# Dealing recombinations and end sums out over units in a hybrid decoder layer

## The chip, the core and the metric

The kernel runs on one core of one Trainium2 chip. A core has a matrix engine (PE), a vector engine (DVE), a scalar engine (ACT), GpSimd (POOL) and a queue engine (SP); POOL and SP issue the DMAs here. The metric is device time in microseconds of one launch, the median of the runs. Lower is better.

## What is computed

One layer of a decoder over 272 positions (16 learned ones and 256 of the sequence) of width 2048, all in float32: a half-step feed-forward block, a mixer (sparse attention beside a short gated convolution), and a second half-step feed-forward block. The change touches the two gates of the mixer and the second feed-forward block:

```python
merged = sigmoid(ga) * y_attn + sigmoid(gc) * y_conv      # ga, gc: columns of u @ w_in
h = h + merged @ w_out
u = rms_norm(h, ffn2_norm_g)
h = h + 0.5 * (silu(u @ w_gate) * (u @ w_up)) @ w_down    # width 5632
return h[:, N_META:]
```

## The kernel before

**Two parts, one stream.** All weights are read once, in the order of their use, by an object `Stream` (`st`). It cuts them into units of at most 1024 float32 columns on 128 partitions. For each unit ACT makes a rounded high part (`whi`, L202) and DVE the rest (`wlo`, L203), so that a product in float32 is three fp32r matmuls (L577 to L579). `st.next()` opens a unit. In this order it runs the functions registered by `st.early` that are due, then `st.split`, which makes the high and low parts of the unit five ahead, and then what was registered by `st.later(fn, lag)`; a lag of 1 is the unit that is opened next (or the one being opened, when the call comes from an early function). Each engine works its own instructions in the order in which the program issues them, so this order is the order of DVE's queue.

**Pairs and banks.** From the gates on (from about 1100 us) a stage is a `group`: 256 tokens against 512 columns of two matrices (gate and up, or two column blocks of the down matrix). The contraction runs over pairs of 128-row blocks. A plain pair (kind `C`) makes 8 block products in two units, 24 matmuls: the first unit (`plain_half`) adds to the PSUM banks q2 and q3, the second to q4 and q8; `hook(n)` stands between the two. A seven-product pair (kind `S` or `D`) makes 7 products in 21 matmuls over four units of 2, 2, 2 and 1 blocks, in the order of banks q7, q5, q6, q3, q1, q4, q2. Sums of weights that it needs (`sb`, L180 and L181) are made on DVE by `sum_ahead`, inside `st.split`, six units ahead. For kind `D` a part of these sums is made by an accumulating DMA that POOL issues (L149). All eight PSUM banks are in use.

**The end of a group.** When the last seven-product pair of a group is over, `recombine` is due at the next unit: ACT copies q1 (`va`, L654), and DVE makes `vv`, `vx`, `vv` again and `ve` from q6, q7, q5 and q5 (L655 to L658), all before that unit's split. That unit is called U0 below. When the last pair is over, `after_end` is due: it adds the plain banks to these (four DVE sums over q2, q3, q4, q8), and what follows depends on the group.

- Gates (`gates`, four groups): four sums (L1131), four sigmoids on ACT.
- `up_group` (eleven groups, g = 0 to 10): four sums in the order q3, q4, q2, q8 (L1270), two SiLU on ACT (L1272), the products (L1277) one unit later. The products are turned by eight PE transposes (`turn_mid`, `turn_four`, L624) into banks and copied out as `mid`. This happens at the hook of pair 6 of the next up group (banks q1 and q5), or at pair 1 of the down group (q6 and q1).
- `down_group`, twice a half: the output `ht` (two tiles of 128 tokens by 2048) takes half of each recombined tile (`after_seven`, four DVE operations L1301, at U0 right behind `recombine`) and half of each bank (four more L1301 in `after_end`). In the last group the output DMAs (L1312) follow.

The plan is up 0 to 3, down, up 4 to 7, down, up 8 to 10, down. The kinds of an up group are `CCCDCDCC` for g = 0 and `DCDCDCCC` else; a half of a down group has `CCDCDCDC` (four up groups) or `CCDCDC` (three), the same in both halves.

**The start of the second block.** In up group 0 the residual `h` is turned to token rows by eight groups of four transposes (`turn_h`, L1251), each into a bank that ACT copies out (L1252): two at the hook of pair 0, four at pair 1, two at pair 2. `norm2` at pair 2 puts the sums of squares into bank q6.

Of the kernel before, what the change touches and what calls it, by code (L numbers as in the profile page):

```python
# [12 lines left out]
ALU = mybir.AluOpType  # L13
# [242 lines left out]
def tile_decoder_layer(  # L256
# [61 lines left out]
            st.add(wo[d, :, a * P : b * P], b - a, P)  # L318
    chunks(wo, SIDE, KD)
    for kind, at in PLAN:  # L320
        for k in [p[0] for p in (pairs_up(at) if kind == "up" else pairs_down(at) * 2)]:
            st.add_pair(k, w2_c, w2_d)

    const.tile([P, 32], F32, name="lead")
# [294 lines left out]
    def turn_four(to, m, tags, extra=None):  # L619

        for j in range(NT):
            ps = bank(tags[j], "pt")
            for f in range(4):
                nc.tensor.transpose(ps[:, f * P : (f + 1) * P], m[j][:, f * P : (f + 1) * P], ident)  # L624

            def after(j=j, ps=ps):
                cols = slice(j * P, (j + 1) * P)
                src = ps.rearrange("p (f t) -> p f t", f=4)
                for a, b, x in to:
                    split_into(x[:, :, 0, cols], x[:, :, 1, cols], src[:, a:b, :])  # L630
                if extra:
                    extra(src, cols)

            st.later(after)

    def group(todo, hook, after_seven, after_end):
# [12 lines left out]
        buf = {}  # L649

        def recombine():
            a, v, x, e = (small_tile(n) for n in "avxe")
            buf.update(q2=a, q3=v, q4=x, q8=e)
            nc.scalar.activation(a, q["q1"][0], AF.Copy)  # L654
            nc.vector.tensor_sub(v, q["q6"][0], a)  # L655
            nc.vector.tensor_add(x, q["q7"][0], v)
            nc.vector.tensor_sub(v, q["q5"][0], v)
            nc.vector.scalar_tensor_tensor(e, q["q5"][0], -1.0, x, op0=ALU.mult, op1=ALU.add)  # L658
            after_seven(buf)

        for n, (kind, four, ts) in enumerate(todo):
            b11, b12, b21, b22 = four()
            if kind != "C":
                t1, t3, t2, t4 = (both(ts()[:, :, f * P : (f + 1) * P]) for f in range(4))
                for tag, t in (
                    ("q7", t3), ("q5", t1), ("q6", t2), ("q3", b22), ("q1", b11), ("q4", t4), ("q2", b21)
                ):
                    mac3(of(tag), t, st.next())
                if n == last:
                    st.early(recombine)  # L670
            else:
                plain_half(b11, b12, b21, b22, of("q2"), of("q3"))
                hook(n)
                plain_half(b11, b12, b21, b22, of("q4"), of("q8"))
        st.early(lambda: after_end(q, buf))

    with ExitStack() as mix:
        a_hi, a_lo = parts(LATER)
# [445 lines left out]
        def gates(c):  # L1124

            box = {}

            def after_end(q, buf):
                box.update(buf)
                for tag in ("q2", "q3", "q4", "q8"):  # L1130
                    nc.vector.tensor_add(buf[tag], q[tag][0], buf[tag])  # L1131
                for n, tag in enumerate(("q2", "q3", "q4", "q8")):
                    j = 1 + n % 2
                    nc.scalar.activation(buf[tag], buf[tag], AF.Sigmoid, scale=rcol[:, 2 * j : 2 * j + 1])
# [77 lines left out]
    def turn_mid(tags):  # L1212
# [3 lines left out]
        g, m = waiting.pop(0)  # L1216
        to = right[0][:, slot[g]]
        mids[g] = to
        ks = [f // 2 for k, gg, f in pairs_down(part[g]) if gg == g and k != "C"]
        if ks:  # L1220
            x = small_tile("m1").rearrange("p (i t) -> p i t", i=2)

# [31 lines left out]
    def up_group(g):  # L1254

        def hook(n):
            if g == 0:
                if n == 0:
                    st.later(lambda: nc.vector.tensor_add(ssq[0][:, META:], ssq[0][:, META:], ssq[1][:, META:]))
                if n == 2:  # L1260
                    norm2()
                if n < 3:
                    for i, tag in zip(((0, 1), (2, 3, 4, 5), (6, 7))[n], ("q1", "q5", "q6", "q7")):
                        turn_h(i // 2, i % 2, tag)
            elif n == 6:
                turn_mid(("q1", "q5"))

        def after_end(q, buf):
            for tag in ("q3", "q4", "q2", "q8"):
                nc.vector.tensor_add(buf[tag], q[tag][0], buf[tag])  # L1270
            for j, tag in enumerate(("q2", "q3")):
                nc.scalar.activation(buf[tag], buf[tag], AF.Silu, scale=r2[:, 2 * j : 2 * j + 1])  # L1272

            def products():
                m = [small_tile(f"m{j}") for j in range(NT)]
# [7 lines left out]

        group(
            [(k, lambda i=i: four_of(act2, 2 * i, 2 * i + 1), lambda i=i: made[i]) for k, i in pairs_up(g)],
            hook, lambda buf: None, after_end,
        )

    PLACES = {"q2": (0, 0), "q3": (1, 0), "q4": (0, 1), "q8": (1, 1)}

    def down_group(gs, final):
        pairs = pairs_down(gs)
        for half in range(2):

            def place(tag, half=half):
# [4 lines left out]
            def add_half(to, x):  # L1300
                nc.vector.scalar_tensor_tensor(to, x, 0.5, to, op0=ALU.mult, op1=ALU.add)  # L1301

            def after_seven(buf, place=place):
                for tag in PLACES:
                    add_half(place(tag)[2], buf[tag])

            def after_end(q, buf, place=place):
                for tag in ("q3", "q4", "q2", "q8"):
# [5 lines left out]
            group(  # L1314
                [
                    (k, lambda g=g, f=f: four_of(mids[g], f, f + 1), lambda g=g, f=f: made_mid[g, f])
                    for k, g, f in pairs
                ],
                lambda n: n == 1 and half == 0 and turn_mid(("q6", "q1")), after_seven, after_end,
            )  # L1320

    right = []
# [63 lines left out]
def _second(wg, wu, wd):  # L1386
    res = []
    for kind, at in PLAN:
        if kind == "up":
            res += [_quads(k, wg, wu, i, at, at) for k, i in pairs_up(at)]  # L1390
        else:
            res += [
                _quads(k, wd, wd, 2 * g + f // 2, 2 * m, 2 * m + 1) for m in range(2) for k, g, f in pairs_down(at)
            ]
    return _both_kinds(res)

# [81 lines left out]
```

## Time and profile before

| | |
|---|---|
| median of 3 runs | 2197.49 us (2193.02 to 2199.24) |
| profiled execution, its own time | 2201.74 us |
| its span | 2200.0 us |
| mean granted PE clock in it | 0.991 |
| DVE, ACT, POOL busy | 1503.8, 1080.3, 82.3 us |
| weights and inputs read | 431.29 MB, 197 GB/s over the span |

The profile gives times from the start of the span. A row of the timeline reads: start, duration, engine, line, operation, output tile<-input tiles, shape, count, and in brackets the idle time of the engine before it with what ended it. A row of the windows view has the busy time and, in brackets, the number of instructions of each engine in a stretch, then the clock that PE was granted and the DMA engines' busy share. Ends of matmuls are modelled, so PE's pace is read from the number of matmuls in a window rather than from its busy time.

### The profile page before, as it was taken

Reading aid. Unit: us, or ns where it says so; the run is one execution under the profiler, and the core shown is the slowest. Engines: PE = TensorE matmul, PEld = TensorE weight load, DVE = VectorE, ACT = ScalarE, POOL = GpSimd, SP = SyncE. Lnnn points to the kernel's source line nnn. Section 1 sums busy time; section 2 is a strip of 40 time slices with the busy share of each in tenths; the row PEclk is TensorE's granted clock in tenths of the full one; section 3 lists DMA queues with packets and bytes.
Section 4 is the critical chain, followed back from the end, with each engine's and each line's share of the span. In section 5 each row is a group of like instructions: output and inputs, shape, how many; then the busy total and the mean of one; then the engine's idle time right before and its main releaser. Section 6 shows DMA issues by size and latency. Waiting matters only on the chain.

```text
span 2200.0 us, 32155 instructions
## 1 busy us (share of the span) xinstructions
PE 2143.0 (97%) x13045; PEld 1926.7 (88%) x13045; DVE 1503.8 (68%) x1918; ACT 1080.3 (49%) x1397; POOL 82.3 (4%) x94
## 2 busy tenths in 40 slices
PE   8999999999999999999999999999998999989997
PEld 8999999999999998889988888888877787777876
DVE  7555544455555555686677885778877887778876
ACT  6444433344444445564455554666554565545643
POOL 2000000000000000000000000100000000000000
PEclk9999999999999999999999999999999999999999
DMA  6555555555545555443555555578777877778764
GB/s 238 190 178 187 173 176 183 178 172 180 185 173 175 184 175 175 153 163 128 179 202 198 187 208 172 192 240 255 240 232 231 253 241 236 221 228 256 239 221 122
DMA packets 77765, 435.48 MB, mean 198 GB/s; under 512 B 8656, under 2 KB 8784, under 8 KB 36912
## 3 DMA queue, kind: packets, MB, share of 16 engines
q1 hardware_dynamic: 70416, 407.67, 52.7%
q0 software_dynamic: 7056, 25.59, 6.9%
q8 instruction: 102, 1.67, 0.3%
q14 instruction: 47, 0.39, 0.0%
q10 hardware_dynamic: 144, 0.17, 0.0%
HBM read 431.29 MB, written 2.10 MB: 197 GB/s over the span
## 4 chain that ended last, share of the span: by engine, by line
PE 85%; DVE 8%; ACT 2%; DMA 2%; issue 1%; POOL 1%; SPq 0%; DVEq 0%; ACTq 0%; POOLq 0%
PE q L577 11%; PE q L578 11%; PE q L579 11%; PE pd L372 4%; PE pd L371 4%; PE pd L373 4%; PE pu L371 4%; PE pg L371 4%; PE pg L373 4%; PE pu L373 4%; PE pu L372 4%; PE pg L372 4%; DVE wlo L203 3%; DMA raw<-in_w2d_dram 2%; ACT whi L202 2%; PE po L386 1%
## 5 line engine op out<-in xcount | busy, mean ns | idle before, releaser
L203 DVE TENSOR_TENSOR wlo<-raw,whi 128x1024 fp32r<-128x1024 f32 (+1 forms) x752 | 903.7, 1208 | 607.5 <-ACT whi L202 591.2
L202 ACT ACTIVATE whi<-raw 128x1024 fp32r<-128x1024 f32 (+1 forms) x752 | 782.8, 1044 | 858.8 <-PE q L579 187.8
L577 PE MATMUL q<-whi,act 128*128 128x512 f32 x833 | 327.1, 393 | 8.0 <-DVE vv L1270 4.1
L578 PE MATMUL q<-wlo,act 128*128 128x512 f32 x833 | 325.5, 391 | 0.8 <-DVE wlo L203 0.8
L579 PE MATMUL q<-whi,act 128*128 128x512 f32 x833 | 325.0, 390 | 0.0
L371 PE MATMUL pd<-mid,whi 128*128 128x272 f32 x704 | 201.7, 287 | 0.0
L372 PE MATMUL pd<-mid,whi 128*128 128x272 f32 x704 | 201.7, 287 | 0.0
L373 PE MATMUL pd<-mid,wlo 128*128 128x272 f32 x704 | 201.7, 287 | 0.0
L577 PEld LDWEIGHTS q<-whi,act 128*128 128x128 f32 x833 | 157.0, 188 | 42.5 <-DVE vv L1270 5.4
L371 PE MATMUL pg<-act,whi 128*128 128x272 f32 x672 | 192.7, 287 | 0.0
L372 PE MATMUL pu<-act,whi 128*128 128x272 f32 x672 | 192.5, 287 | 0.0
L373 PE MATMUL pg<-act,wlo 128*128 128x272 f32 x672 | 192.5, 287 | 0.0
L371 PE MATMUL pu<-act,whi 128*128 128x272 f32 x672 | 192.5, 287 | 0.0
L372 PE MATMUL pg<-act,whi 128*128 128x272 f32 x672 | 192.5, 287 | 0.0
L373 PE MATMUL pu<-act,wlo 128*128 128x272 f32 x672 | 192.5, 287 | 0.0
L578 PEld LDWEIGHTS q<-wlo,act 128*128 128x128 f32 x833 | 157.0, 188 | 33.6 <-DVE wlo L203 1.9
L579 PEld LDWEIGHTS q<-whi,act 128*128 128x128 f32 x833 | 156.9, 188 | 32.9
L577 PE MATMUL q<-whi,mid 128*128 128x512 f32 x272 | 111.5, 410 | 29.9 <-DVE ht L1301 20.5
L371 PEld LDWEIGHTS pd<-mid,whi 128*128 128x128 f32 x704 | 132.6, 188 | 0.0
L372 PEld LDWEIGHTS pd<-mid,whi 128*128 128x128 f32 x704 | 132.6, 188 | 0.0
L373 PEld LDWEIGHTS pd<-mid,wlo 128*128 128x128 f32 x704 | 132.6, 188 | 0.0
L371 PEld LDWEIGHTS pg<-act,whi 128*128 128x128 f32 x672 | 126.6, 188 | 0.0
(289 smaller groups left out, 3777.7 us busy)
## 6 DMA issues: line engine op xcount, KB each, us to landing
raw<-in_wgu_dram SPq DMA_DIRECT2D x87, 1024.0 KB, 4.8
raw<-in_w_dram SPq DMA_DIRECT2D x84, 1024.0 KB, 5.0
raw<-in_w2d_dram SPq DMA_DIRECT2D x96, 512.0 KB, 5.5
raw<-in_wd_dram SPq DMA_DIRECT2D x44, 1024.0 KB, 4.8
raw<-in_wg_dram SPq DMA_DIRECT2D x32, 1024.0 KB, 4.8
raw<-in_wcv_dram SPq DMA_DIRECT2D x24, 1024.0 KB, 4.8
raw<-in_w2d_dram POOLq DMA_DIRECT2D x48, 512.0 KB, 5.7
raw<-in_wb_dram SPq DMA_DIRECT2D x16, 1024.0 KB, 4.9
```

Of the source, the lines that this page charges most:

```text
L202: nc.scalar.activation(to[0], raw, AF.Copy)
L203: nc.vector.tensor_sub(to[1], raw, to[0].bitcast(F32))
L371: nc.tensor.matmul(ps, whi, xhi, start=first, stop=False)
L372: nc.tensor.matmul(ps, whi, xlo, start=False, stop=False)
L373: nc.tensor.matmul(ps, wlo, xhi, start=False, stop=last)
L386: nc.tensor.matmul(ps.rearrange("p (a t) -> p a t", a=2), whi, x(i), start=i == 0, stop=False)
L577: nc.tensor.matmul(ps, xhi, whi, start=n == 0, stop=False)
L578: nc.tensor.matmul(ps, xhi, wlo, start=False, stop=False)
L579: nc.tensor.matmul(ps, xlo, whi, start=False, stop=n == total - 1)
```

## The change

1. `recombine` keeps its ACT copy at U0, and its four DVE operations go out one by one, behind the splits of U0, U0+1, U0+2 and U0+3. The four additions to `ht` in a down half follow behind the splits of U0+4 (two) and U0+5 (two).
2. `after_end` is called twice: for q2 and q3 ahead of the second unit of the group's last pair, for q4 and q8 ahead of the unit after that pair. Sigmoids and SiLU go one unit behind their sums.
3. In down halves the second half gets kinds of its own: `CDCDCDCC` and `CDDCCC`.
4. Turned tiles use banks q6 and q1 at pair 6 in place of q1 and q5. In `turn_four` the ACT copies for later sums (`extra`, L1225) come ahead of the high and low parts.
5. In up group 0 four groups of transposes stand at pair 1 (q1, q5, q6, q7), none at pair 0, and four at pair 2 behind `norm2` (q1, q5, q7, and q1 again).
6. An output DMA is issued when both additions to its part of `ht` are out.

```diff
-def pairs_down(gs):
+def pairs_down(gs, half):
     a = list(gs)
     if len(a) > 3:
-        kinds, at = "CCDCDCDC", [(0, 2), (1, 2), (0, 0), (2, 2), (1, 0), (3, 0), (2, 0), (3, 2)]
+        kinds, at = [
+            ("CCDCDCDC", [(0, 2), (1, 2), (0, 0), (2, 2), (1, 0), (3, 0), (2, 0), (3, 2)]),
+            ("CDCDCDCC", [(0, 2), (0, 0), (1, 2), (1, 0), (2, 2), (2, 0), (3, 0), (3, 2)]),
+        ][half]
     else:
-        kinds, at = "CCDCDC", [(0, 2), (1, 2), (0, 0), (2, 0), (1, 0), (2, 2)]
+        kinds, at = [
+            ("CCDCDC", [(0, 2), (1, 2), (0, 0), (2, 0), (1, 0), (2, 2)]),
+            ("CDDCCC", [(0, 2), (0, 0), (1, 0), (1, 2), (2, 0), (2, 2)]),
+        ][half]
...
             def after(j=j, ps=ps):
+                if extra:
+                    extra(src, cols)
                 for a, b, x in to:
                     split_into(x[:, :, 0, cols], x[:, :, 1, cols], src[:, a:b, :])
-                if extra:
-                    extra(src, cols)
...
             nc.scalar.activation(a, q["q1"][0], AF.Copy)
-            nc.vector.tensor_sub(v, q["q6"][0], a)
-            nc.vector.tensor_add(x, q["q7"][0], v)
-            nc.vector.tensor_sub(v, q["q5"][0], v)
-            nc.vector.scalar_tensor_tensor(e, q["q5"][0], -1.0, x, op0=ALU.mult, op1=ALU.add)
-            after_seven(buf)
+            st.later(lambda: nc.vector.tensor_sub(v, q["q6"][0], a), 1)
+            st.later(lambda: nc.vector.tensor_add(x, q["q7"][0], v), 2)
+            st.later(lambda: nc.vector.tensor_sub(v, q["q5"][0], v), 3)
+            st.later(
+                lambda: nc.vector.scalar_tensor_tensor(e, q["q5"][0], -1.0, x, op0=ALU.mult, op1=ALU.add), 4
+            )
+            if after_seven:
+                for i, tag in enumerate(buf):
+                    st.later(lambda tag=tag: after_seven(tag, buf[tag]), 5 + i // 2)
...
                 plain_half(b11, b12, b21, b22, of("q2"), of("q3"))
+                if n == len(todo) - 1:
+                    st.early(lambda: after_end(q, buf, ("q2", "q3")))
                 hook(n)
                 plain_half(b11, b12, b21, b22, of("q4"), of("q8"))
-        st.early(lambda: after_end(q, buf))
+        st.early(lambda: after_end(q, buf, ("q4", "q8")))
...
-                lambda n: n == 6 and c > 0 and turn_merged(("q1", "q5")), lambda buf: None, after_end,
+                lambda n: n == 6 and c > 0 and turn_merged(("q6", "q1")), None, after_end,
...
+                if n == 1:
+                    for i, tag in enumerate(("q1", "q5", "q6", "q7")):
+                        turn_h(i // 2, i % 2, tag)
                 if n == 2:
                     norm2()
-                if n < 3:
-                    for i, tag in zip(((0, 1), (2, 3, 4, 5), (6, 7))[n], ("q1", "q5", "q6", "q7")):
-                        turn_h(i // 2, i % 2, tag)
+                    for i, tag in enumerate(("q1", "q5", "q7", "q1")):
+                        turn_h(2 + i // 2, i % 2, tag)
             elif n == 6:
-                turn_mid(("q1", "q5"))
+                turn_mid(("q6", "q1"))
...
-            def after_seven(buf, place=place):
-                for tag in PLACES:
-                    add_half(place(tag)[2], buf[tag])
-
-            def after_end(q, buf, place=place):
-                for tag in ("q3", "q4", "q2", "q8"):
-                    j, c, to = place(tag)
-                    add_half(to, q[tag][0])
-                    if final:
-                        nc.sync.dma_start(out[j * P : (j + 1) * P, c : c + WIDE], to)
+                met[tag] += 1
+                if final and met[tag] == 2:
+                    nc.sync.dma_start(out[j * P : (j + 1) * P, c : c + WIDE], to)
+
+            def after_end(q, buf, tags, add_half=add_half):
+                for tag in tags:
+                    add_half(tag, q[tag][0])
```

More of the change, by code (lines that the diff above doesn't have):

```diff
@@ L320, in tile_decoder_layer @@
     for kind, at in PLAN:
-        for k in [p[0] for p in (pairs_up(at) if kind == "up" else pairs_down(at) * 2)]:
+        for k in [p[0] for p in (pairs_up(at) if kind == "up" else pairs_down(at, 0) + pairs_down(at, 1))]:
             st.add_pair(k, w2_c, w2_d)
@@ L1126, in gates, with after_end, sigmoids @@
             box = {}
-            def after_end(q, buf):
-                box.update(buf)
-                for tag in ("q2", "q3", "q4", "q8"):
+            def after_end(q, buf, tags):
+                for j, tag in enumerate(tags):
                     nc.vector.tensor_add(buf[tag], q[tag][0], buf[tag])
-                for n, tag in enumerate(("q2", "q3", "q4", "q8")):
-                    j = 1 + n % 2
-                    nc.scalar.activation(buf[tag], buf[tag], AF.Sigmoid, scale=rcol[:, 2 * j : 2 * j + 1])
+                    box[tag] = buf[tag]
+                def sigmoids():
+                    for j, tag in enumerate(tags):
+                        nc.scalar.activation(buf[tag], buf[tag], AF.Sigmoid, scale=rcol[:, 2 + 2 * j : 3 + 2 * j])
+                st.later(sigmoids, 2)
             group(
                 [(k, lambda i=i: four_of(act1, 2 * i, 2 * i + 1), lambda i=i: made1[i]) for k, i in pairs_gate(c)],
-                lambda n: n == 6 and c > 0 and turn_merged(("q1", "q5")), lambda buf: None, after_end,
+                lambda n: n == 6 and c > 0 and turn_merged(("q6", "q1")), None, after_end,
             )
@@ L1218, in turn_mid @@
         mids[g] = to
-        ks = [f // 2 for k, gg, f in pairs_down(part[g]) if gg == g and k != "C"]
+        ks = [f // 2 for k, gg, f in pairs_down(part[g], 0) if gg == g and k != "C"]
         if ks:
@@ L1259, in hook, with after_end, silus @@
                     st.later(lambda: nc.vector.tensor_add(ssq[0][:, META:], ssq[0][:, META:], ssq[1][:, META:]))
+                if n == 1:
+                    for i, tag in enumerate(("q1", "q5", "q6", "q7")):
+                        turn_h(i // 2, i % 2, tag)
                 if n == 2:
                     norm2()
[L1262 to L1264 removed]
+                    for i, tag in enumerate(("q1", "q5", "q7", "q1")):
+                        turn_h(2 + i // 2, i % 2, tag)
             elif n == 6:
[L1266 to L1269 removed]
+                turn_mid(("q6", "q1"))
+        def after_end(q, buf, tags):
+            for tag in tags:
                 nc.vector.tensor_add(buf[tag], q[tag][0], buf[tag])
[L1271 to L1272 removed]
+            def silus():
+                for j, tag in enumerate(tags):
+                    nc.scalar.activation(buf[tag], buf[tag], AF.Silu, scale=r2[:, 2 * j : 2 * j + 1])
+            if tags == ("q2", "q3"):
+                st.later(silus, 2)
+                return
             def products():
@@ L1285, in up_group @@
             [(k, lambda i=i: four_of(act2, 2 * i, 2 * i + 1), lambda i=i: made[i]) for k, i in pairs_up(g)],
-            hook, lambda buf: None, after_end,
+            hook, None, after_end,
         )
@@ L1291, in down_group @@
     def down_group(gs, final):
-        pairs = pairs_down(gs)
         for half in range(2):
+            pairs = pairs_down(gs, half)
             def place(tag, half=half):
@@ L1298, in place, with add_half @@
                 return j, c, ht[j][:, c : c + WIDE]
-            def add_half(to, x):
+            met = dict.fromkeys(PLACES, 0)
+            def add_half(tag, x, place=place, met=met):
+                j, c, to = place(tag)
                 nc.vector.scalar_tensor_tensor(to, x, 0.5, to, op0=ALU.mult, op1=ALU.add)
-            def after_seven(buf, place=place):
-                for tag in PLACES:
-                    add_half(place(tag)[2], buf[tag])
-            def after_end(q, buf, place=place):
-                for tag in ("q3", "q4", "q2", "q8"):
-                    j, c, to = place(tag)
-                    add_half(to, q[tag][0])
-                    if final:
-                        nc.sync.dma_start(out[j * P : (j + 1) * P, c : c + WIDE], to)
+                met[tag] += 1
+                if final and met[tag] == 2:
+                    nc.sync.dma_start(out[j * P : (j + 1) * P, c : c + WIDE], to)
+            def after_end(q, buf, tags, add_half=add_half):
+                for tag in tags:
+                    add_half(tag, q[tag][0])
             group(
@@ L1318, in down_group @@
                 ],
-                lambda n: n == 1 and half == 0 and turn_mid(("q6", "q1")), after_seven, after_end,
+                lambda n: n == 1 and half == 0 and turn_mid(("q6", "q1")), add_half, after_end,
             )
@@ L1392, in _second @@
             res += [
-                _quads(k, wd, wd, 2 * g + f // 2, 2 * m, 2 * m + 1) for m in range(2) for k, g, f in pairs_down(at)
+                _quads(k, wd, wd, 2 * g + f // 2, 2 * m, 2 * m + 1) for m in range(2) for k, g, f in pairs_down(at, m)
             ]
```

## The prediction

> **What bounds the kernel now.** I read the page, then what PE waited for, then PE by windows, then DVE's timeline at the ends of groups.
>
> ```profile
> span 2200.0 us, 32155 instructions
> PE 2143.0 (97%) x13045; PEld 1926.7 (88%) x13045; DVE 1503.8 (68%) x1918; ACT 1080.3 (49%) x1397; POOL 82.3 (4%) x94
> ```
>
> ```profile
> PE q L577 <- DVE ht L1301: 23.9, 5, 6.8
> PE q L577 <- DVE va L1270: 9.4, 3, 4.2
> ...
> PE q L577 <- DVE vv L1270: 4.1, 2, 2.7
> ```
>
> PE is the bound, and the change takes no matmul away. What it can win is time in which PE stands. The rows of what it waited for (total us, times, longest) are all at ends of groups: a bank that the next group writes has not been read yet. How much each stop costs, the slow clock behind it included, I read from the number of matmuls in a window around it.
>
> ```profile
> 1439.00:1453.00 14.00, 11.54 (x56) 0.88 0.83 248
> 1572.00:1584.00 12.00, 10.58 (x47) 1.00 0.71 207
> 1616.00:1626.00 10.00, 7.38 (x26) 0.83 0.49 150
> 1663.00:1675.00 12.00, 5.17 (x15) 0.72 0.61 178
> 1714.00:1726.00 12.00, 10.31 (x45) 1.00 0.75 222
> 1844.00:1856.00 12.00, 9.34 (x35) 0.86 0.73 216
> 1889.00:1899.00 10.00, 7.39 (x26) 0.83 0.53 154
> 1936.00:1948.00 12.00, 5.17 (x15) 0.72 0.69 200
> 1987.00:1999.00 12.00, 10.31 (x46) 1.00 0.76 223
> 2115.00:2127.00 12.00, 7.81 (x24) 0.72 0.47 132
> 2154.00:2166.00 12.00, 5.17 (x14) 0.72 0.87 245
> ```
>
> ```profile
> 2000.00:2060.00 60.00, 60.00 (x267) 1.00 0.83 264
> ```
>
> The last row is an undisturbed stretch: 60/267 = 0.2247 us a matmul. So 12 us hold 53.4 matmuls and 10 us hold 44.5. The matmuls missing, times 0.2247:
>
> - between the halves of a down group (1663, 1936, 2154): 38.4, 38.4 and 39.4 missing, 8.6 + 8.6 + 8.9 = **26.1 us**;
> - up to down (1616, 1889, 2115): 18.5, 18.5 and 29.4, 4.2 + 4.2 + 6.6 = **15.0**;
> - down to up (1714, 1987): 8.4 and 7.4, 1.9 + 1.7 = **3.6**;
> - up to up (1572, 1844): 6.4 and 18.4, 1.4 + 4.1 = **5.5**;
> - start of the second block (1439, where transposes spoil the count): 2.5 of wait (row further below), and (1 - 0.88) x 14 = 1.7 of clock, **4.2**.
>
> Together 54.4 us, 2.5%. The gates have no such stop.
>
> The clock belongs to it: it stays 1.00 where PE stood least (the rows of 1572, 1714, 1987, with waits under 1.8 us: 23.9 less 3 x 6.8 leaves 3.5 for two), and falls to 0.72 to 0.88 behind waits from 2.5 us. The Trainium skill (TensorE: Matmul & The Clock Gate, What's actually happening) says that the half clock comes back after an idle window of about 3.4 us. By that rule the 2.5 us wait of 1439 would cost no clock and its term would be 2.5 in place of 4.2; the rows show the loss already there, so I go by the rows.
>
> **Part by part.** First the long stop, on DVE's timeline.
>
> ```profile
> 1659.42 0.68 DVE L655 TENSOR_TENSOR vv<-q,va 128x512 f32<-128x512 f32 x1
> ...
> 1665.80 2.35 DVE L203 TENSOR_TENSOR wlo<-raw,whi 128x1024 fp32r<-128x1024 f32 x2
> 1668.07 2.48 DVE L1301 SCALAR_TENSOR_TENSOR ht<-q,ht 128x512 f32<-128x512 f32 x4
> ```
>
> PE needs q2 and q3 at the start of the next half. They were final half a pair before that, but DVE first works off four recombinations, four additions, two sums and two low parts (1659.42 to 1668.07), one behind the other.
>
> *Between halves.* Now q2 and q3 are added ahead of the last pair's second unit (2 x 0.6 us, while PE fills q4 and q8 for 12 x 0.2247 = 2.7 us), and q4 and q8 have the next pair's first unit, again 2.7 us, for 1.2 us of work. Stop gone: 26.1. What is late next is q5: the next half's first seven-product pair reads it as its second block, at U0+4 plus 3 matmuls, and `ve`, its last reader, stands behind the split of U0+3.
>
> ```profile
> L202 ACT ACTIVATE whi<-raw 128x1024 fp32r<-128x1024 f32 (+1 forms) x752 | 782.8, 1044 | 858.8 <-PE q L579 187.8
> ```
>
> Counted from the start of U0+3: PE is there after 2.7 + 0.7 = 3.4 us; `ve` comes behind a high part (1.04, and some 0.3 for the hand-overs, an estimate), a low part (1.2) and its own 0.7, 3.2 to 3.3 us. That is a draw. I put 0.3 us a time, **25.1** in all; bounds: nothing lost (26.1), or one more sum pair and low part ahead of it (1.3 + 1.2 us and the clock, about 4 each: 14).
>
> *Up to down.* Same release, a C pair comes first: 4.2 + 4.2 gone. At 2115 DVE itself was late, since it stood until 2112.74 for an accumulated weight:
>
> ```profile
> 2112.74 0.69 DVE L180 TENSOR_TENSOR sb<-raw 128x512 f32<-128x512 f32 x1 [1.97 <-DMA raw<-in_w2d_dram]
> ...
> 2118.53 0.68 DVE L1270 TENSOR_TENSOR va<-q,va 128x512 f32<-128x512 f32 x1
> ```
>
> The additions of q2 and q3 now stand behind two sums and one low part: 2112.74 + 1.34 + 1.17 + 1.3 = 2116.6 in place of 2119.2, and PE wants them at about 2114.9 (its longest wait on `va`, 4.2, before the end of that row). A stop of 1.8 to 1.9 stays, too short for the clock. **13.1** of 15.0.
>
> *Down to up.* q3 comes free in time. Here the seven-product pair follows at U0+4, so again the draw at q5: **3.1** of 3.6 (bounds 3.6 and -5).
>
> *Up to up.* Here the change can cost. In groups 1, 2, 5, 6 and 9 the next group begins with a D pair, whose sums (`sb`) are issued inside the split of U0. Today all four recombinations are ahead of them; afterwards `vv`, which frees q6, is behind the sums and a low part. Where the accumulating DMA is late, DVE stands at the sums, and the transposes at pair 6 now go into q6.
>
> ```profile
> 1520.34 0.93 PE L624 MATMUL pt<-ident,vm 128*128 128x128 f32 x7
> 1563.09 1.04 PE L624 MATMUL pt<-ident,vm 128*128 128x128 f32 x8
> 1832.78 1.04 PE L624 MATMUL pt<-ident,vm 128*128 128x128 f32 x8
> ```
>
> ```profile
> 1518.63 0.69 DVE L180 TENSOR_TENSOR sb<-raw 128x512 f32<-128x512 f32 x1 [1.97 <-DMA raw<-in_w2d_dram]
> 1562.74 0.69 DVE L180 TENSOR_TENSOR sb<-raw 128x512 f32<-128x512 f32 x1 [3.33 <-DMA raw<-in_w2d_dram]
> 1564.08 2.35 DVE L203 TENSOR_TENSOR wlo<-raw,whi 128x1024 fp32r<-128x1024 f32 x2
> 1834.38 0.69 DVE L180 TENSOR_TENSOR sb<-raw 128x512 f32<-128x512 f32 x1 [5.28 <-DMA raw<-in_w2d_dram]
> ```
>
> From the start of the sums `vv` ends 1.34 (to the low part) + 1.17 (half of 2.35) + 0.68 = 3.2 us later: 1521.8, 1565.9, 1837.6. The transposes stood at 1520.34, 1563.09, 1832.78, so PE waits 1.5, 2.8 and 4.8 us; the second shrinks to 1.3, as PE is already 1.5 later. Groups 5 and 9 have their weights in time. Sum 7.6, and 2.4 of clock behind the long one (2115: 4.2 waited, 6.6 lost). The old stops go, 5.5, partly since the copies of `extra` no longer wait for DVE. Net **-4.5**. Bounds: +5.5, if the accumulates come as fast as their fastest; 5.5 - 5 x 7.2 = -30, if all five groups are like group 6.
>
> ```profile
> DMA to landing us min/median/max: 5.3/5.7/11.5
> ```
>
> *Start of the second block.* The stop at pair 1 goes, 4.2 us.
>
> ```profile
> 1448.19 3.13 PE L1251 MATMUL pht<-ident,h 128*128 128x128 f32 x16 [2.46 <-ACT ht L1252]
> ```
>
> These 16 transposes would start at about 1444.7, without the 2.5 and without pair 0's eight (some 1.0, half of what 16 take at full clock); 2.0 for themselves and 24 matmuls (5.4) later, at 1452.1, `norm2` wants q6, whose copy by ACT is the third of the first row here:
>
> ```profile
> 1452.52 2.04 ACT L1252 ACTIVATE ht<-pht 128x512 f32<-128x512 f32 x4
> ...
> 1459.94 0.58 ACT L1252 ACTIVATE ht<-pht 128x512 f32<-128x512 f32 x1
> ```
>
> ACT was behind DVE there, so the time of this row stays, and PE waits about 2 us. Then q1 is taken twice at one hook: the last four transposes wait for ACT to copy the first, behind a high part and `norm2`'s root, about 2.4 us. 4.2 - 4.4, and perhaps some clock: **-1** (bounds +4 and -4).
>
> *Tail.* The last DVE row below is the end of 12 operations in one queue; PE's last matmul starts at 2194.46.
>
> ```profile
> 2193.78 2.47 DVE L1301 SCALAR_TENSOR_TENSOR ht<-q,ht 128x512 f32<-128x512 f32 x4
> 2194.46 0.39 PE L579 MATMUL q<-whi,mid 128*128 128x512 f32 x1
> ```
>
> Only q4 and q8 stay behind the last matmul: 2194.9 + 0.7 = 2195.6 in place of 2196.25, **+0.6**. The recombinations were hidden behind matmuls already.
>
> *At nothing:* the gates. PE had no stop there, and nothing but the order changes; their cover is the branch products (96 matmuls, 21.6 us) before q2 is wanted again. The instruction counts of every engine stay as they are, and so do the loads.
>
> Sum: 25.1 + 13.1 + 3.1 - 4.5 - 1 + 0.6 = **36.4 us**. The profiled execution took 2201.74 (1.74 around its span), 4.25 over the median; it would become 2165.3. From the median, 2197.49 - 36.4 = **2161.1**.
>
> **Rivals.**
>
> 1. *Everything comes in time.* Without stops at the moved places: 26.1 + 15.0 + 3.6 + 5.5 + 2.1 (half of the start's 4.2) + 0.6 = 52.9, **2144.6**. For it: `vv` is late only where a DMA is. Against it: the sums waited on it in three of five such groups.
> 2. *Late accumulates in all five groups.* 25.1 + 13.1 + 3.1 - 30 - 1 + 0.6 = 10.9, **2186.6**. For it: the lost stops gave the DMA engines rest (0.47 to 0.69 busy in most of these windows, against 0.83 in the undisturbed one), which is gone. The Trainium skill (SBUF — State Buffer, SBUF: two separate sides) has another cause, DVE keeping POOL from writing descriptors, by which a fuller DVE would make all accumulates late. In the row of 1562.74 DVE was idle for 3.33 us and the accumulate was late all the same, so this trace does not support it as the cause.
> 3. *q5 is the new stop.* `ve` one sum pair and two low parts late (1.34 + 2.35 + 1.7 of clock = 5.4) in five places (three between halves, two down to up): 36.4 - 27 + 1.5 = 10.9, again **2186.6**. Against it: DVE is 68% busy.
> 4. *Slower.* The mechanism of the second, sharper: sums that hold `vv`, q6 and the transposes in groups 1, 2, 5, 6 and 9. All other terms and the old stops come to 46.4, so the kernel is slower from 46.4 / 5 = 9.3 us a group on, a wait of 6.9 with 2.4 of clock, against 4.8 in the worst row. At 9 us of wait, 5 x 11.4 = 57: **2208**.
> 5. *It doesn't do what it says:* the early sums of q2 and q3 still stand behind a low part whose buffer is late, and the stops stay: about **2197**.
>
> **Chances.** Forecast 0.50 (2152 to 2172), first rival 0.18, second 0.12, third 0.11, slower 0.04, no effect 0.05. The range 2142 to 2182 holds the forecast and the first rival, and those of the second and third in which about half as many places are hit. About 0.3% (6.6 us) can be told from no change here. Faster: 0.50 + 0.18 + 0.21 of the middle rivals' 0.23 = 0.89; same 0.06; slower 0.05.
>
> **What would show it.** Right: no wait of PE on `ht` (L1301) over 1 us, clock 1.00 between the halves, PE's waits on `va` down to one of about 2 us. For the up groups: transposes L624 that wait for the first recombination, in groups 1, 2 and 6, with DVE standing at L180 before it. For the start: a wait of `norm` or `pht` on ACT's copies at pair 2. Wrong if PE's waits on DVE keep their sum under other names (`ve` first), or if accumulates land 3 us later than they do now.

## The result and the profile after

The changed kernel takes 2158.75 us (2157.47 to 2160.50), the kernel before, measured with it, 2195.26 us (2192.80 to 2199.24). The ratio is 0.9833, 95% interval 0.9813 to 0.9852: 36.5 us less. The profiled execution took 2159.46 us. One run of experiment 5 took 2549.41 us at a granted clock of 0.78, and the figures there are of its four other runs.

From the page of the changed kernel: span, and busy time of the engines.

```profile
span 2157.7 us, 32167 instructions
PE 2130.6 (99%) x13045; PEld 1917.0 (89%) x13045; DVE 1500.2 (70%) x1918; ACT 1082.2 (50%) x1397; POOL 82.1 (4%) x94
```

The number of matmuls is the same and DVE's work too; PE stands less. What PE waited for behind 1430 us in the changed kernel (total us, times, longest us); up to there the two traces run side by side:

```profile
PE q L583 <- DVE ht L1327: 4.9, 3, 1.7
PE q L583 <- DVE ve L665: 2.7, 3, 1.3
PE norm L1256 <- ACT ht L1267: 2.1, 1, 2.1
PE pht L1266 <- ACT ht L1267: 1.7, 1, 1.7
```

The 6.8 us stops on `ht` are down to 1.7, the waits on `va` and `vv` are gone, `ve` and the two ACT waits at the start of the second block are new. The same places as in the prediction's rows, now by windows of the changed kernel (after the window: PE, PEld, DVE, ACT and POOL busy with counts, granted clock, DMA share, GB/s):

```profile
1574.00:1586.00 12.00, 12.00 (x55) 9.94 (x53) 11.86 (x17) 8.30 (x10) 0.87 (x1) 1.00 0.62 151
1612.00:1624.00 12.00, 11.88 (x53) 9.54 (x52) 10.73 (x17) 6.23 (x8) 0.87 (x1) 1.00 0.73 221
1659.00:1671.00 12.00, 10.26 (x45) 7.81 (x44) 11.96 (x18) 4.51 (x5) 0.87 (x1) 1.00 0.81 236
1914.00:1926.00 12.00, 10.33 (x45) 7.88 (x44) 11.97 (x18) 4.41 (x6) 0.88 (x1) 1.00 0.92 260
1958.00:1970.00 12.00, 10.67 (x48) 8.46 (x47) 11.96 (x16) 5.83 (x6) 0.87 (x1) 1.00 0.86 259
2080.00:2092.00 12.00, 12.00 (x54) 9.73 (x53) 11.02 (x17) 6.16 (x8) 0.87 (x1) 1.00 0.84 249
2118.00:2130.00 12.00, 9.38 (x40) 6.91 (x39) 11.96 (x17) 3.66 (x5) 0.00 (x0) 1.00 0.52 192
```

```profile
1455.50:1462.30 6.80, 5.08 (x17) 3.92 (x16) 2.81 (x5) 3.90 (x7) 0.00 (x0) 0.50 0.68 217
```

Read as there, 53.4 matmuls make 12 full us. Between the halves (1659, 1914, 2118) 8.4, 8.4 and 13.4 matmuls are missing, 1.9 + 1.9 + 3.0 = 6.8 us in place of 26.1; the third window holds a wait on `ve` of 1.1 us too. Up to down (1612, 2080) nothing to speak of, down to up (1958; the other one, from 1703, is full) 5.4 matmuls, 1.2 us. Up to up (1574; the other one, from 1832, has 55 matmuls too) nothing is left, but the step from group 0 to group 1 has a wait on `ve` of 0.3 us. The clock is 1.00 everywhere but in the last row, 6.8 us at half clock at the start of the second block: 3.4 us lost in clock and waits of 2.1 + 1.7, partly the same time. Between the halves the windows of before had 14 or 15 matmuls where there are 40 to 45 now.

| term | forecast | measured |
|---|---|---|
| between halves | +25.1 | 26.1 - 6.8 = +19.3 |
| up to down | +13.1 | +15.0 |
| down to up | +3.1 | 3.6 - 1.2 = +2.4 |
| up to up | -4.5 | 5.5 - 0.3 = +5.2 |
| start of the second block | -1 | 4.2 - 6.3 = -2.1 |
| tail | +0.6 | 5.5 - 4.5 = +1.0 |
| sum | 36.4 | 40.8 |

For the start, 6.3 is the two waits and the clock outside the second of them, some 2.5. The tail runs from the start of the last matmul to the end of the span: 2194.46 to 2200.0 before, 2153.23 to 2157.7 after. The two profiled executions differ by 42.3 us, so 1.5 have no place here. The count explains about that much: a full window of 12 us holds 55 matmuls, not 53.4, since it counts those that straddle its ends, so each of the five places with nothing left was put some 0.3 us too low (an estimate, (55 - 53.4) x 0.2247). The execution profiled before lay 6.5 above the median of its runs and the one after 0.7 above its own, which is why the medians differ by less.

### The profile page after: what moved, and what is told of

The parts are those of the page before. It is cut to its first block, busy times and chain, and to the rows that moved or that the text cites. A ratio compares the mean times of both kernels' runs of the same rounds, so it can differ in the third digit from the quotient of the medians.

```text
span 2157.7 us, 32167 instructions
## 1 busy us (share of the span) xinstructions
PE 2130.6 (99%) x13045; PEld 1917.0 (89%) x13045; DVE 1500.2 (70%) x1918; ACT 1082.2 (50%) x1397; POOL 82.1 (4%) x94
## 4 chain that ended last, share of the span: by engine, by line
PE 90%; DVE 4%; DMA 3%; ACT 1%; POOL 1%; issue 0%; SPq 0%; DVEq 0%; POOLq 0%; ACTq 0%
PE q L583 11%; PE q L584 11%; PE q L585 11%; PE pd L378 4%; PE pd L377 4%; PE pd L379 4%; PE pu L377 4%; PE pg L377 4%; PE pg L379 4%; PE pu L379 4%; PE pu L378 4%; PE pg L378 4%; DMA raw<-in_w2d_dram 3%; DVE wlo L209 2%; PE po L392 2%; PE pbr L583 1%
## 5 line engine op out<-in xcount | busy, mean ns | idle before, releaser
L377 PEld LDWEIGHTS pg<-act,whi 128*128 128x128 f32 x672 | 126.6, 188 | 0.0
L378 PEld LDWEIGHTS pg<-act,whi 128*128 128x128 f32 x672 | 126.6, 188 | 0.0
```

Of the source, the lines that this page charges most:

```text
L377: nc.tensor.matmul(ps, whi, xhi, start=first, stop=False)
L378: nc.tensor.matmul(ps, whi, xlo, start=False, stop=False)
```

## The experiments

The experiments ask which of the change's parts brought the gain, why the up groups gained where a loss was forecast, and what holds PE in the places left. Every kernel here computes the whole result. The kernel before had medians of 2196.4 us beside experiments 1, 2, 5 and 6, 2195.27 beside 3, 4, 8 and 9, and 2195.01 beside 7, 10 and 11. Parts 3 (but for the place of one pair, experiment 5) and 6 of the change and the banks of part 4 were not undone by themselves.

### 1. Recombinations and additions at once again

```diff
-            st.later(lambda: nc.vector.tensor_sub(v, q["q6"][0], a), 1)
-            st.later(lambda: nc.vector.tensor_add(x, q["q7"][0], v), 2)
...
+            nc.vector.tensor_sub(v, q["q6"][0], a)
+            nc.vector.tensor_add(x, q["q7"][0], v)
...
             if after_seven:
-                for i, tag in enumerate(buf):
-                    st.later(lambda tag=tag: after_seven(tag, buf[tag]), 5 + i // 2)
+                for tag in buf:
+                    after_seven(tag, buf[tag])
```

> The changed kernel, but the four recombinations and the four additions to the output stand together at U0 again, ahead of that unit's split; q2 and q3 are still added half a pair early. My theory: the accumulates of the up groups land in time because the end sums no longer stand in front of the next group's splits, so here too DVE stands at its sums (second block's sb) under 1 us in groups 1, 2, 5 and 6, no transpose waits, and the waits on ve (2.7 us) go. Between the halves q2 and q3 again stand behind eight operations (5 us): waits of 3 to 4 us with the clock behind them, three times some 5.5 against 1.8 now. Time about 2168 (2163 to 2174). Rival, that dealing the recombinations out is what made the accumulates timely: sums late by 2 to 5 us in groups 1, 2 and 6 as in the kernel before, 2174 to 2180.

Measured: 2180.05 us (2178.70 to 2180.84), ratio 0.9925 [0.9909, 0.9940]. Waits of PE in it:

```profile
PE q L583 <- DVE ht L1325: 22.3, 5, 7.5
```

The long stops between the halves are back, though q2 and q3 are still added half a pair early: eight operations now stand ahead of those additions. 21.3 us of the 36.5 hang on dealing them out. The time expected by my theory (2163 to 2174) was too low: it came out at the end of the rival's range (2174 to 2180). The rival's mechanism is seen in part. In groups 4, 5, 6 and 8 the accumulated weights landed 6.1 to 7.5 us after the start of U0 (ACT's copy of q1); in the changed kernel they land 1.0 to 2.0 us after it in every up group from 1 on that another up group follows. But no transpose waits for it here. Between the halves DVE stands 2.2 to 3.4 us for an accumulate besides, so these stops are not the eight operations alone; experiment 11 takes the two apart.

### 2. All four plain banks added at the end again

```diff
-                if n == len(todo) - 1:
-                    st.early(lambda: after_end(q, buf, ("q2", "q3")))
...
-        st.early(lambda: after_end(q, buf, ("q4", "q8")))
+        st.early(lambda: (after_end(q, buf, ("q2", "q3")), after_end(q, buf, ("q4", "q8"))))
```

> The changed kernel, but q2 and q3 are added together with q4 and q8 after the last pair; recombinations stay dealt out. My theory: this is the part that holds the gain at up to down and that keeps the accumulates in time. Waits of 2 to 3 us at the three steps up to down (4.2 each with the clock), at the between-halves places 3 us each and more, and the accumulates for the next group late again in groups 1, 2 and 6 (DVE idle over 2 us at the sums, waits of the transposes at pair 6 of 1.5 to 5 us): about 2188 (2180 to 2196). Rival, timeliness from dealing out: the same stops at group ends, but no late sums in the up groups and no waiting transposes: about 2178.

Measured: 2179.6 us (2173.45 to 2181.85), ratio 0.9917 [0.9899, 0.9935]. Below the expected range (2180 to 2196), near the rival's 2178; but the late sums and waiting transposes, which the rival did without, are there. Here is the wait that the prediction had forecast for the changed kernel. First DVE's timeline, then PE's, in group 2:

```profile
1564.02 0.69 DVE L186 TENSOR_TENSOR sb<-raw 128x512 f32<-128x512 f32 x1 [5.95 <-DMA raw<-in_w2d_dram]
...
1566.49 0.68 DVE L661 TENSOR_TENSOR vv<-q,va 128x512 f32<-128x512 f32 x1
```

```profile
1567.23 1.97 PE L630 MATMUL pt<-ident,vm 128*128 128x128 f32 x8 [2.68 <-DVE vv L661]
```

DVE stands 5.95 us for the accumulate, `vv` is behind the sums, and the transposes wait 2.68 us for it and then run at half clock (1.97 us for eight in place of 1.04). The same wait stands in groups 5 and 6, 1.3 and 2.0 us. So the mechanism is real; what differs between this kernel and the changed one is when the accumulates land (here 3.6 to 7.3 us after the start of U0 in the same groups). DVE's waits on them behind 1430 us, in this kernel and then in the changed one (total us, times, longest):

```profile
DVE sb L186 <- DMA raw<-in_w2d_dram: 46.0, 17, 5.9
```

```profile
DVE sb L186 <- DMA raw<-in_w2d_dram: 16.6, 14, 2.6
```

### What makes an accumulate late

The rows of issues say more. Group 1: POOL's and SP's queue in the kernel before, then in the changed one.

```profile
1509.73 0.87 POOL L149 DMA_DIRECT2D raw<-in_w2d_dram  x1 [18.66 <-DMA raw<-in_w2d_dram]
...
1509.96 0.33 SPq L154 DMA_DIRECT2D raw<-in_w_dram  x1
```

```profile
1510.89 0.87 POOL L155 DMA_DIRECT2D raw<-in_w2d_dram  x1 [18.64 <-DMA raw<-in_w2d_dram]
...
1512.62 0.33 SPq L160 DMA_DIRECT2D raw<-in_w_dram  x1
```

Before, SP's next load (1024 KB) went out 0.23 us behind the accumulate (512 KB), which took 8.88 us to land, at 1518.61. After, the load goes out 1.73 us behind it, and the accumulate takes 5.42 us, to 1516.31. All 48 accumulates of each kernel sort by this:

| kernel | a load from 2.5 us ahead to 0.5 us behind: cases, median us | none: cases, median us |
|---|---|---|
| before | 12, 8.8 | 36, 5.6 |
| changed | 18, 8.4 | 30, 5.7 |
| experiment 1 | 17, 8.9 | 31, 5.8 |
| experiment 2 | 21, 8.8 | 27, 5.7 |

So a load issued with the accumulate seems to cost it 3 us. Taken over all places, the changed kernel has more late accumulates than the kernel before (18 against 12), and DVE's waits on them are 16.6 us in place of 14.5; but the longest is 2.6 us in place of 5.3. At the five ends of up groups where the prediction looked (1, 2, 5, 6 and 9), they were issued 1.7 to 3.6 us before the start of U0 and took 6.6 to 11.5 us; now they are issued 3.8 to 4.7 us before it, with no load near, and take 5.4 to 6.7. The Trainium skill (DMA: Bandwidth & Descriptors, Issuing engines are not separate DMA queues) says that DMAs of all issuing engines run on the same 16 DMA engines and interleave; the table fits that, but does not show where the two meet. To test the cost, a *hold*: POOL writes one column of the next load's buffer, which the load then overwrites. POOL gets to it only behind the accumulate, and SP's load must wait for it.

```diff
             raw = pool.tile([P, RAW], F32, name="raw")
+            if self.sum_pool and self.n_loaded and self.loads[self.n_loaded - 1][1] > RAW:
+                self.nc.gpsimd.memset(raw[:, :1], 0.0)
             if n > RAW:
```

### 3 and 4. The hold in experiment 2's kernel and in the changed kernel

> The kernel with all end sums after the last pair (the second experiment), and one thing more: the weight load that follows a D pair's loads waits until POOL has issued that pair's accumulating DMA (a one-column POOL memset of the buffer, which the load overwrites). My theory: an accumulate is late when the next 1 MB load is issued before it or with it. In the second experiment, 25 of 48 accumulates had that, median 8.65 us to landing, against 5.72 for the other 23. So nearly all land in 5.5 to 6 us here, DVE's idle time at the sums falls from 46 us to under 15, the transposes at pair 6 no longer wait for the first recombination (5.9 us now), and the time is 8 to 12 us less, about 2169. Rival: accumulates are late because they are issued late against PE's place, or because the DMA engines are full; then they stay at 8 us or the loads held back come late themselves (waits of high parts on loads): 2180 or more.

> The changed kernel with the same hold: the load behind a D pair's loads waits for the issue of its accumulate. My theory: the waits left between the halves (ht, 4.9 us) and on ve (2.7 us) come from late accumulates (8 to 9 us to landing there) and go, about 2152. Rival: the queue of DVE is what keeps them: they stay, 2157 to 2160; or held loads come late: above 2160.

Measured: experiment 2 with the hold 2160.25 us (2158.43 to 2162.94), ratio 0.9841 [0.9821, 0.9861], 19 us less than without; 8 to 12 were expected, so the theory had the direction and not the size. The changed kernel with the hold **2151.55 us** (2150.97 to 2154.04), ratio 0.9802 [0.9783, 0.9822], 7.2 us less than the changed kernel, as expected (2152). In the second, POOL and SP in group 1:

```profile
1510.95 0.87 POOL L157 DMA_DIRECT2D raw<-in_w2d_dram  x1 [16.37 <-DVE wlo L211]
1513.06 0.10 POOL L153 MEMSET raw<- 128x1 f32 x1 [1.24 <-issue]
...
1513.19 0.33 SPq L162 DMA_DIRECT2D raw<-in_w_dram  x1
```

No load is left in the near column in either (0 of 48), and the accumulates take 5.6 us in the median, at most 6.4 in the changed kernel with the hold (issue to landing; rows of the changed kernel with the hold and without it below). In experiment 2's kernel with the hold one still took 9.5, with no load near, so a load near them is not the only thing that delays them.

```profile
DMA to landing us min/median/max: 5.2/5.6/6.4
```

```profile
DMA to landing us min/median/max: 5.3/6.9/10.8
```

DVE's waits on them in the changed kernel with the hold, and what is left there of PE's waits at the ends of groups:

```profile
DVE sb L188 <- DMA raw<-in_w2d_dram: 1.9, 5, 0.7
```

```profile
PE q L585 <- DVE ve L667: 1.1, 1, 1.1
```

16.6 us have become 1.9, and one stop remains. In experiment 2's kernel the wait of the transposes is gone. So the late accumulate was the cause of these waits, and keeping the load behind it landed it in time there. Whether the two share DMA engines or something else was not measured by itself.

### 5. The second D pair of the long second halves one place later

```diff
-            ("CDCDCDCC", [(0, 2), (0, 0), (1, 2), (1, 0), (2, 2), (2, 0), (3, 0), (3, 2)]),
+            ("CCDCDDCC", [(0, 2), (1, 2), (0, 0), (2, 2), (1, 0), (2, 0), (3, 0), (3, 2)]),
```

> The changed kernel with CCDCDDCC in place of CDCDCDCC in the second half of the two long down groups: its first seven-product pair comes one C pair later, the last one stays. My theory: the waits left between those halves (1.7 each, on ht) and at the second step down to up (1.3, on ve) come from a sum pair that now stands at U0-2 and waits for its accumulate, which keeps the first recombination and the sums of q2 and q3 behind it. With the pair later the sums stand behind them: the two waits on ht go under 0.3, time 4 to 5 us less, 2154. Rival, that DVE's queue is just too full there: the waits stay or move into the two D pairs in a row (waits on wlo), 2158 to 2162.

Measured: 2155.88 us (2154.74 to 2157.52), ratio 0.9814 [0.9800, 0.9827], 2.9 us less than the changed kernel by medians where 4 to 5 were expected; the intervals overlap. The trace is clearer. In the changed kernel DVE's timeline between the halves is:

```profile
1655.34 0.69 DVE L186 TENSOR_TENSOR sb<-raw 128x512 f32<-128x512 f32 x1 [2.05 <-DMA raw<-in_w2d_dram]
1656.07 0.69 DVE L187 TENSOR_TENSOR sb<-sb,last 128x512 f32<-128x512 f32 x1
1656.68 2.35 DVE L209 TENSOR_TENSOR wlo<-raw,whi 128x1024 fp32r<-128x1024 f32 x2
1658.95 1.22 DVE L209 TENSOR_TENSOR wlo<-sb,whi 128x1024 fp32r<-128x1024 f32 x1
1660.08 0.68 DVE L661 TENSOR_TENSOR vv<-q,va 128x512 f32<-128x512 f32 x1
1660.68 1.28 DVE L1327 SCALAR_TENSOR_TENSOR ht<-q,ht 128x512 f32<-128x512 f32 x2
```

The change brings the second half's first D pair forward by one place, its sums are due just ahead of the end, and they wait 2.05 us for their accumulate. The additions of q2 and q3 (last row) are behind them. With the D pair later PE's waits on `ht` fall from 4.9 to 1.8 us:

```profile
PE q L583 <- DVE ht L1327: 1.8, 3, 1.4
```

The 1.4 is the short half, which this experiment leaves alone. So the stop left between the halves comes from the new order of pairs, through an accumulate; with the hold no wait on `ht` is left in the order of the change either.

### 6 and 7. The turned tiles of the start spread out, without and with the hold

```diff
-                if n == 1:
-                    for i, tag in enumerate(("q1", "q5", "q6", "q7")):
-                        turn_h(i // 2, i % 2, tag)
...
-                    for i, tag in enumerate(("q1", "q5", "q7", "q1")):
-                        turn_h(2 + i // 2, i % 2, tag)
+                at, tags = {1: (0, ("q1", "q5", "q7")), 6: (3, ("q6", "q1")), 7: (5, ("q7", "q6", "q1"))}.get(n, (0, ()))
+                for i, tag in enumerate(tags, at):
+                    turn_h(i // 2, i % 2, tag)
```

> The changed kernel with the transposes of the residual in up group 0 at other places: three at pair 1 (q1, q5, q7), norm2 alone at pair 2 (q6, not used before), two at pair 6 (q6, q1) and three at pair 7 (q7, q6, q1). My theory: the two waits at pair 2 (2.1 on ACT's copy of q6, 1.7 on the copy of q1) and the half clock behind them go, 3.8 + about 2: 2153. Rival: ACT was behind at that place anyway and the wait comes back as one on high parts or at the end of group 0 (q5 or q7 not copied in time): 2157 to 2160.

> The changed kernel with the hold and with the transposes of up group 0 at pairs 1, 6 and 7 (the fourth experiment). There the transposes at pair 6 waited 8.0 us for the first recombination, which stood behind sums that waited 6.1 us for an accumulate. My theory: with the accumulate in time this wait falls under 2 us, and the waits at pair 2 stay away: 2147 (2145 to 2150), the fastest of all. Rival: DVE's lag at the start of the second block holds the first recombination by itself: a wait of 3 us or more at pair 6, 2151 or more.

What the second text calls the fourth experiment is number 6. Measured, for 6: 2165.76 us (2164.71 to 2168.70), ratio 0.9860 [0.9847, 0.9874], a miss: 7 us more than the changed kernel. Both waits on ACT are gone, but at pair 6 the transposes now want q6, and `vv` is late. PE's timeline:

```profile
1482.26 1.97 PE L1266 MATMUL pht<-ident,h 128*128 128x128 f32 x8 [7.97 <-DVE vv L661]
```

With the hold (7) this wait is 3.1 us, and the kernel takes 2150.70 (2149.64 to 2154.20), ratio 0.9800 [0.9776, 0.9823]: within 1 us of the changed kernel with the hold, where the start costs two waits. The theory (under 2 us, 2147) missed, and the wait is the one of the rival (3 us or more): the accumulate explains 4.9 of the 8.0 us, and no gain is to be told.

### 8 and 9. Two small parts undone

`extra` behind the high and low parts again (8), and the places of `turn_h` as before (9):

```diff
-                if extra:
-                    extra(src, cols)
                 for a, b, x in to:
                     split_into(x[:, :, 0, cols], x[:, :, 1, cols], src[:, a:b, :])
+                if extra:
+                    extra(src, cols)
```

```diff
-                if n == 1:
-                    for i, tag in enumerate(("q1", "q5", "q6", "q7")):
-                        turn_h(i // 2, i % 2, tag)
...
-                    for i, tag in enumerate(("q1", "q5", "q7", "q1")):
-                        turn_h(2 + i // 2, i % 2, tag)
+                if n < 3:
+                    for i, tag in zip(((0, 1), (2, 3, 4, 5), (6, 7))[n], ("q1", "q5", "q6", "q7")):
+                        turn_h(i // 2, i % 2, tag)
```

> The changed kernel, but in the turning of the products the ACT copies for later sums stand behind the high and low parts again, as before. I put a part of the gain in the up groups down to their move. If that is right, ACT and DVE wait for each other again (DVE idle 1 us before each second low part of mid, some 8 us in all), and where DVE is late anyway the sums slip: 2160 to 2164, with DVE standing longer at the sums of groups 1, 2, 5 and 6. Rival: DVE has that microsecond to spare and nothing moves: 2157 to 2160.

> The changed kernel, but the transposes of the residual in up group 0 stand where they stood before (two groups at pair 0, four at pair 1, two at pair 2). My working gave the new places a loss of 1 us; the trace shows waits of 2.1 and 1.7 and a half clock of 6.8 us behind them against 2.5 and 3.4 before. Expected: one wait of about 2.5 us on ACT's copy at pair 1, none at pair 2, time 1 to 3 us less, 2156 to 2158. Rival: the new places are no loss, since DVE's lag there is the limit: 2158 to 2161.

Measured: 2162.78 us (2161.99 to 2163.54), ratio 0.9851 [0.9832, 0.9870], for the first, 4 us more than the changed kernel, as expected; the sums are late again in groups 2 and 6 (3.8 and 3.4 us), but not in 1 and hardly in 5 (0.8 us). For the second 2160.95 (2158.84 to 2165.52), ratio 0.9846 [0.9825, 0.9868]: one wait of 3.8 us in place of 2.1 and 1.7, and no difference that can be told; the 1 to 3 us less that were expected did not come. The loss forecast for the start is too small to be shown by times.

### 10. The kernel before with the hold

> The kernel before, with nothing but the hold: the load behind a D pair's loads waits until POOL has issued the accumulate. It tells how much of the change's 36 us a timely accumulate alone gives. My theory: it takes the stops up to up (5.5) and the long part of the one at up group 10 to down (some 2.4 and clock), and DVE's idle time at the sums (14.5 us) nearly all; the stops between halves stay, as their cause is eight operations and low parts in DVE's queue ahead of the sums of q2 and q3: PE waits on ht 20 us or more, time about 2187 (2183 to 2190). Rival: late accumulates are behind most of the stops: 2175 or less.

Measured: 2189.89 us (2187.36 to 2191.84), ratio 0.9970 [0.9959, 0.9982], as expected. The waits on `vv` are gone and the wait of 4.2 us on `va` is 2.6; the long stops are what they were:

```profile
PE q L579 <- DVE ht L1303: 23.9, 5, 6.8
```

So accumulates in time bring about 5 us here. They can't be the main part of the change's gain.

### 11. Experiment 1's kernel with the hold

> The changed kernel with the hold, but recombinations and their additions together at U0. It tells what dealing them out is worth by itself, once accumulates land in time. My theory: between the halves eight operations (4.9 us) and a low part stand ahead of the sums of q2 and q3, which PE wants 5.4 us after U0: three waits of about 2 us on ht, one or two of 1 us down to up, none up to up: about 2159 (2156 to 2162) against 2151.6. Rival: dealing out only mattered through the accumulates: 2151 to 2154.

Measured: 2166.30 us (2164.91 to 2167.65), ratio 0.9864 [0.9841, 0.9887]; the effect was expected, its size not, by 7 us. Its waits of PE, and DVE's timeline between the halves:

```profile
PE q L585 <- DVE ht L1327: 12.7, 3, 4.6
```

```profile
1656.23 0.68 DVE L663 TENSOR_TENSOR vv<-q,va 128x512 f32<-128x512 f32 x1
...
1661.29 1.22 DVE L211 TENSOR_TENSOR wlo<-sb,whi 128x1024 fp32r<-128x1024 f32 x1
1662.42 1.28 DVE L1327 SCALAR_TENSOR_TENSOR ht<-q,ht 128x512 f32<-128x512 f32 x2
```

All eight operations and a low part, 6.2 us, stand ahead of the additions for which PE waits, with no accumulate in it. Put together (medians, us):

| | without hold | with hold |
|---|---|---|
| before | 2195.3 | 2189.9 |
| not dealt out, q2 and q3 early | 2180.1 | 2166.3 |
| dealt out, q2 and q3 late | 2179.6 | 2160.3 |
| dealt out, q2 and q3 early (the change) | 2158.8 | 2151.6 |

With the hold, dealing out brings 14.8 us and the early additions 8.7. Without it 21.3 and 20.9: the difference, some 7 and 12 us, is the accumulates, which are late when either part is missing.

## Why the prediction was right, and where not

**The bound and the stops.** Right. PE was the bound, the stops at the ends of groups were what could be won, and three quarters of it were: of 54.4 us counted, 14.3 are left (6.8 + 1.2 + 6.3). The order of the kernels in the table fits the cause given, additions of q2 and q3 queued behind work that nobody waits for.

**Between halves, 25.1 forecast, 19.3 measured.** The mechanism held, the size did not. Of the five draws at q5 (three between halves, two down to up), forecast at 0.3 us each, two were lost, by 1.1 and 1.3 us (`ve`); its third wait, 0.3 us, is at the start of group 1. The 0.3 us of hand-overs in that sum came from no row: in both traces a low part that waits for its high part starts 0.03 us behind it. What was missed is the third part of the change: the earlier D pair sets its sums, and their accumulate, ahead of the additions of q2 and q3. That is "one more sum pair and low part ahead of it", which stood there as a bound, but of q5, not of q2; the clock that this bound charged wasn't lost, as waits stayed at 1.7. The forecast "no wait on `ht` over 1 us" fell by it.

**Up to down, 13.1 and 15.0.** (By its own figures the stop that stays is 2116.6 - 2114.9 = 1.7, not 1.9; and 26.1 less three times 0.3 is 25.2, 3.6 less twice 0.3 is 3.0. These slips nearly cancel.) The 1.9 us that were to stay came from an accumulate late at 2112.74. At the same place the sums now wait 0.88 us (at 2082.59) instead of 1.97; the additions of q2 and q3 behind them end at 2086.34 (2085.66 + 0.68), just ahead of the down group's first matmul at 2086.44.

**Up to up, -4.5 and +5.2.** This is the step that failed, by 10 us. It took each landing from the rows of before and asked what stands behind it. But landings move with the queues: an accumulate's time hangs on when SP's next load goes out, and here the accumulates of all five groups went out 0.9 to 2.1 us earlier against U0, with no such load within 1 us. That they did so because buffers came free earlier would fit, but was not measured by itself. The step itself is sound, experiment 2 shows it at work (2.68 us at 1567.23), only its input was wrong. In the changed kernel none of the five groups' accumulates lands later than 2.0 us after the start of U0 (before: up to 9.3). The forecast row to look for, transposes that wait for `vv`, is not in the changed kernel. The bound of +5.5, "as fast as their fastest", is nearly what came.

**Start, -1 and -2.1.** Both waits are there as forecast, 2.1 and 1.7 us; "some clock" was 3.4 us in a 6.8 us stretch.

**Tail, down to up.** As forecast within 0.4 and 0.7 us.

**The total.** 36.4 forecast, 36.5 between the medians. That it fits so closely is chance: +9.7 (up to up), +1.9, +0.4, -5.8, -1.1 and -0.7 come to +4.4, and the rest is the choice of execution. The first rival (everything in time, 2144.6) was nearer in the up groups than the forecast; with the hold, which the change doesn't have, the kernel comes within 7 us of it. The second rival's cause, the DMA engines' rest gone, is not what happened: they were busier at most of the ends (0.73 to 0.92), and the accumulates at the up groups' ends came earlier all the same.

**The cause of late accumulates.** The Trainium skill (SBUF — State Buffer, SBUF: two separate sides) was weighed there for DVE blocking POOL; it says so of DVE operations in a 2-port performance mode, and no run here shows in which mode these ran. The hold leaves DVE's work as it is (1500.7 us busy, 1500.2 without) and moves the median from 6.9 to 5.6, so DVE's load doesn't explain it.

**The clock.** To go by the rows was right: in experiment 2 the clock halved behind a wait of 2.68 us. The Trainium skill (TensorE: Matmul & The Clock Gate, What's actually happening) has about 3.4 us of idling for it, and here shorter waits were enough. But what the prediction read from the rows, nothing lost under 1.8 us and something from 2.5 us on, is no threshold either. In experiment 9 a wait of 1.87 us (it ends at 1662.20) was followed by 3.4 us at half clock, while in experiment 2 the clock stayed at 1.00 behind waits of 2.38 and 2.03 us (they end at 1455.28 and 1459.29). The windows of the two:

```profile
1660.00:1668.00 8.00, 6.13 (x21) 4.66 (x20) 6.83 (x11) 1.69 (x2) 0.00 (x0) 0.79 0.99 314
```

```profile
1454.00:1466.00 12.00, 8.69 (x48) 7.39 (x49) 6.74 (x14) 9.26 (x15) 0.00 (x0) 1.00 0.61 180
```

What decides between them is not shown.

## What to carry to other kernels

Where an engine works in order, look at what the bottleneck engine waits for and at everything queued ahead of it: put the operations that release a buffer first and deal the others out over later steps. When a forecast rests on the moment at which a DMA lands, don't carry that moment over from the old trace; ask which issues it shares its time with, and whether the change moves them. Here a transfer on which a queue stands was given the lead by one cheap write that holds the next load back.

## What the runs showed of the hardware

An accumulating DMA of 512 KB took 8.4 to 8.9 us in the median when a load of 1024 KB was issued from 2.5 us ahead of it to 0.5 us behind it, and 5.6 to 5.8 when none was (48 accumulates in each of four kernels). A one-column write on POOL of 0.10 us between the two was worth 5 us in the kernel before, 7 in the changed kernel, 14 in experiment 1's and 19 in experiment 2's. The granted clock of PE halved for 3.4 or 6.8 us behind some waits of 1.9 us and more, and not behind others of up to 2.4.
